# Two-layer mLSTM block on one core: the 512 tokens of x in four chunks of 128 instead of two of 256

## The chip, the core and the metric

The program runs on one core of a Trainium2 chip. Its engines, by the names of the profile, are PE (matrix multiply, with PEld for its weight loads), DVE (vector), ACT (scalar: exponentials, copies with a scale), POOL, and SP, which here only issues DMAs. The metric is the device time of one launch in microseconds; lower is better.

## The reference, cut to what matters

Two layers of a block mix 512 tokens of `x` and 256 tokens of a prefix `ctx` (width 1024). A layer projects both with `w_in`, runs an mLSTM (4 heads of width 128, forward and backward), a Fourier mixer and a convolution, joins them with `w_out`, and adds an MLP. The mLSTM is written as a scan over chunks:

```python
D = bcum[..., :, None] - bcum[..., None, :] + li[..., None, :]      # masked to s <= t
m_t = max(bcum + m, max(D))
S   = (q k^T) * exp(D - m_t)                                        # inside the chunk
num = exp(bcum + m - m_t) * (C q) + S v                             # state C, then the chunk
den = exp(bcum + m - m_t) * (n q) + sum(S)
h   = num / max(|den|, exp(-m_t))
C_new = exp(...) * C + sum_s exp(g_s - m_new) v_s k_s^T             # state for the next chunk
```

The backward direction is the same on reversed tokens. The result doesn't depend on the chunk length (but for rounding): a longer chunk has more of `S`, a shorter one more states `C`. In the last layer only x is needed after the mLSTM, and ctx only gives its state.

## The kernel before

Tokens stand as 2 blocks of 128 of ctx and 4 blocks of x. Work is recorded layer by layer. In a layer the columns of `w_in` go by chunks of 128 (`CHUNKS`): t and a for the convolution, then q, k, o for heads 0 to 3, then the Fourier columns. The products of a chunk are L464 (three matmuls for each of 8 slices of the weight and each token range, 48 in the first layer where both ranges are needed). After the chunk o of head h a generator `mlstm(h, ...)` is staged; `advance()` (called after the next chunks) runs its first part up to the first `yield` (scores, states), then its second (outputs), then its third (transposes back, L785). `background()` slips matmuls of another projection (L248, which fill one PSUM tile over 8 steps) and, by way of the priorities, the taps of the convolution (L690, on DVE) between them.

A scheduler turns the record into a fixed order for each engine. Each engine works its list strictly in that order, and an instruction at the head of the list that has to wait holds all behind it. Tiles come from pools of a fixed size; an instruction that opens a new tile waits until the readers of the tile whose room it takes are done. The pool `aux` has 4 PSUM tiles, and all of scores, transposes, states and outputs of the mLSTM take theirs there; so do the L248 sums, one tile for a long time.

For x, a head of the kernel before does this (first part of `mlstm`):

- `mb`: running maxima, broadcast to all partitions by DMA (L828).
- L835, L841: transposes of k; ACT writes them scaled, into `kw` (ctx, L838, 4 copies) and `kx` (x, L843, 4 copies).
- L848: `qs`, 4 exponentials of 256 columns, and L850 times q.
- `weighted`, once for each chunk of 256: 6 score matmuls of 256 columns (L801, operands rounded to float32r, high and low parts), then 4 exponentials (two of 256 columns, two of 128; L811), 4 masks on POOL (L779), 4 products on DVE (L814).
- L855: state at the start of x, 4 matmuls of 129 columns, copied by ACT to `cs` (L857). L862: 4 more for the second state; DVE combines both (L866).

The second part (L884) takes for each block and direction one state matmul and one or two matmuls inside the chunk, 2.5 on average, so 20 a head for x. Ctx has 6 more in the first layer. The matmuls of L855, L862 and L884 have float32 operands; the trace shows each as two records.

Ahead of that, once a layer, four small DMAs fetch the maxima at the chunk edges from DRAM (`m0`, `m1`, L652 and L653: 4 values of 4 bytes to each of 128 partitions). DVE subtracts them for `dec` (L670).

Of the kernel before, what the change touches and what calls it, by code (L numbers as in the profile page):

```python
# [10 lines left out]
F32 = mybir.dt.float32  # L11
F32R = mybir.dt.float32r
AF = mybir.ActivationFunctionType
# [5 lines left out]
CTX = 256  # L19
# [32 lines left out]
CH = 256  # L52
# [13 lines left out]
def build(tc, a):  # L66
# [408 lines left out]
    def layer(l, res, nbg, first=None):  # L475
# [168 lines left out]
        mdv = md[l][:].rearrange("(d h) t -> h d t", d=2)  # L644


        m0 = small.tile([128, 2, 4], F32, tag="m0", name=nm("m0"))
        m1 = small.tile([128, 2, 4], F32, tag="m1", name=nm("m1"))
        dec = small.tile([128, 2, 4], F32, tag="dec", name=nm("dec"))
        wx = small.tile([128, 4, 4], F32, tag="wx", name=nm("wx"))  # L650
        for d, t0, t1 in ((0, CTX - 1, CTX + CH - 1), (1, 0, CTX + CH)):
            dma(m0[:, d, :], md[l][4 * d:4 * d + 4, t0].partition_broadcast(128))  # L652
            dma(m1[:, d, :], md[l][4 * d:4 * d + 4, t1].partition_broadcast(128))  # L653

        def gate_columns():
            for q in range(2):
                ps = aux()
                for i in range(3):
                    T.transpose(ps[:, 128 * i:128 * i + 128], pm[:, 128 * (3 * q + i):128 * (3 * q + i) + 128], ident)
                v4 = ps[:, :384].rearrange("p (b g d n) -> p b g d n", b=3, g=2, d=2)  # L660
                for i in range(3):
                    V.tensor_copy(pcol[:, 3 * q + i], v4[:, i, 0, :, 0:4])
                    S.activation(em[:, 3 * q + i], v4[:, i, 1, :, 0:4], AF.Exp, scale=-1.0)
            for j in range(CB):
                V.tensor_tensor(wc[:, j], pcol[:, j], m0, ALU.subtract)
            S.activation(wc, wc, AF.Exp)
            for i in range(4):
                V.tensor_tensor(wx[:, i], pcol[:, CB + i, i // 2], m1[:, i // 2], ALU.subtract)
            S.activation(wx, wx, AF.Exp)
            V.tensor_tensor(dec, m0, m1, ALU.subtract)  # L670
            S.activation(dec, dec, AF.Exp)

        y = {}
# [117 lines left out]
        def mlstm(h, q, k, to):  # L791
            y[h] = t3()
            groups = []
            qh, ql, kh, kl = [t3(F32R) for _ in range(4)]
            i0 = XQ if last else 0
            for src, hi, lo in ((q, qh, ql), (k, kh, kl)):
                split(src[:, i0:QW], hi[:, i0:QW], lo[:, i0:QW], True)

            def scores(out, kc, q0, n):
                for i, (kp_, qp) in enumerate(((kh, qh), (kh, ql), (kl, qh))):  # L800
                    T.matmul(out, kp_[:, kc:kc + 128], qp[:, q0:q0 + n], start=i == 0, stop=i == 2)  # L801

            def weighted(mb, kc, q0, blk):

                qk = aux()
                E = t4().rearrange("p (j d t) -> p j d t", j=2, d=2)
                for j in range(2):
                    scores(qk[:, CH * j:CH * j + CH], kc + 128 * j, q0, CH)
                for j, d in ((0, 0), (0, 1), (1, 0), (1, 1)):
                    lo, hi = (128 * j, CH) if d == 0 else (0, 128 * j + 128)  # L810
                    S.activation(E[:, j, d, lo:hi], mb[:, d, lo:hi], AF.Exp, scale=-1.0,  # L811
                                 bias=pcol[:, blk + j, d, h:h + 1])
                    masked(E[:, j, d, 128 * j:128 * j + 128], d == 0)
                    V.tensor_tensor(E[:, j, d, lo:hi], E[:, j, d, lo:hi], qk[:, CH * j + lo:CH * j + hi], ALU.mult)  # L814
                return E

            def within(E, b, blk, d):
                i = b - blk
                js = range(0, i + 1) if d == 0 else range(i, 2)
                return [(E[:, j, d, 128 * i:128 * i + 128], vt[h][:, blk + j, :]) for j in js]  # L820

            if not last:
                mb = c2().rearrange("p (d t) -> p d t", d=2)
                dma(mb, mdv[h, :, 0:CTX].partition_broadcast(128))
                Ec = weighted(mb, 0, 0, 0)
                groups.append((0, range(CB), lambda b, d: within(Ec, b, 0, d)))
            mb = t4().rearrange("p (d t) -> p d t", d=2)
            dma(mb, mdv[h, :, CTX:TOK].partition_broadcast(128))  # L828

            kt = t4()  # L830
            kw = kt[:, 0:512].rearrange("p (d j n) -> p d j n", d=2, j=CB)
            kx = kt[:, 512:1024].rearrange("p (i n) -> p i n", i=4)
            kp = aux()
            for j in range(CB):
                T.transpose(kp[:, 128 * j:128 * j + 128], k[:, 128 * j:128 * j + 128], ident)  # L835
            for d in range(2):
                for j in range(CB):
                    S.activation(kw[:, d, j, :], kp[:, 128 * j:128 * j + 128], AF.Copy, scale=wc[:, j, d, h:h + 1])  # L838
            kp = aux()
            for i in range(4):  # L840
                T.transpose(kp[:, 128 * i:128 * i + 128], k[:, XQ + 128 * i:XQ + 128 * i + 128], ident)  # L841
            for i in range(4):
                S.activation(kx[:, i, :], kp[:, 128 * i:128 * i + 128], AF.Copy, scale=wx[:, i, h:h + 1])  # L843
            qs = t4().rearrange("p (d t) -> p d t", d=2)
            for d in range(2):
                for c in range(2):
                    m_ = m0 if c == d else m1
                    S.activation(qs[:, d, CH * c:CH * c + CH], mb[:, d, CH * c:CH * c + CH], AF.Exp, scale=-1.0,  # L848
                                 bias=m_[:, d, h:h + 1])
            V.tensor_tensor(qs, qs, q[:, XQ:XQ + SEQ].unsqueeze(1).to_broadcast([128, 2, SEQ]), ALU.mult)  # L850
            Ex = [weighted(mb[:, :, CH * c:CH * c + CH], XQ + CH * c, XQ + CH * c, CB + 2 * c) for c in range(2)]
            cp = aux()
            for d in range(2):
                for j in range(CB):
                    T.matmul(cp[:, 129 * d:129 * d + 129], kw[:, d, j, :], vt[h][:, j, :], start=j == 0, stop=j == CB - 1)  # L855
            cs = c2()[:, :258]
            S.activation(cs, cp[:, :258], AF.Copy)  # L857
            cp = aux()
            for d in range(2):
                for j in range(2):  # L860
                    i = 2 * d + j
                    T.matmul(cp[:, 129 * d:129 * d + 129], kx[:, i, :], vt[h][:, CB + i, :], start=j == 0, stop=j == 1)  # L862
            cs1 = c2()[:, :258]
            for d in range(2):
                dd = slice(129 * d, 129 * d + 129)
                V.scalar_tensor_tensor(cs1[:, dd], cs[:, dd], dec[:, d, h:h + 1], cp[:, dd], ALU.mult, ALU.add)  # L866

            def x_terms(b, d):
                s0 = 128 * (b - CB)
                c = (b - CB) // 2  # L870
                return [(qs[:, d, s0:s0 + 128], (cs if c == d else cs1)[:, 129 * d:129 * d + 129])] + \
                    within(Ex[c], b, CB + 2 * c, d)
            groups.append((CTX, range(CB, NB), x_terms))
            yield
            hns = []
            for t0, bs, terms in groups:
                hn = c2()
                ba = tiny.tile([128, 4, 2], F32, tag="ba", name=nm("ba"))
                for i, b in enumerate(bs):
                    ps = aux()  # L880
                    for d in range(2):
                        ts = terms(b, d)
                        for n, (st_, mv) in enumerate(ts):
                            T.matmul(ps[:, 129 * d:129 * d + 129], st_, mv, start=n == 0, stop=n == len(ts) - 1)  # L884
# [592 lines left out]
```

## Time and profile before

| | us |
|---|---|
| runs shown | 1517.34, 1513.02, 1516.81; median 1516.81 |
| profiled execution | 1513.57 |
| its span, first to last instruction | 1511.9 |
| PE busy | 1471.7 (97% of the span) |
| DVE, ACT, POOL busy | 1093.8 (72%), 757.9 (50%), 84.4 (6%) |

The mLSTM of the first layer lies between about 160 and 320 us, that of the last between about 995 and 1115 us. A row of a timeline may merge several equal instructions: "x12" is their number and the second column the time from the first start to the last end, so that the step from one to the next is that time less the length of one, over the number less one, or simply the distance to the next row over the number. The records of PE and ACT overlap: the next instruction starts before the one ahead of it has ended.

### The profile page before, as it was taken

What the parts mean: (1) busy time and instruction counts of PE and PEld (TensorE: products, weight loads), DVE (VectorE), ACT (ScalarE), POOL (GpSimd) and SP (SyncE); (2) the same over time, 40 slices, a digit from 0 to 9 for tenths busy, and PEclk for the clock granted to TensorE, in tenths of its full rate; (3) what the DMA queues carried; (4) which work ended last, traced back from release to release, by engine and by line L of the source; (5) the groups of instructions that cost most, each with busy time, mean ns of one, the idle gap of its engine ahead of it and who ended that gap; (6) DMA issues with size and microseconds to landing.
All of it is one profiled execution on the core that took longest, in us unless ns stands there. A gap on an engine that the chain in (4) does not pass through costs nothing. (4 is left out here: it accounts for less than half of the span.)

```text
span 1511.9 us, 23296 instructions
## 1 busy us (share of the span) xinstructions
PE 1471.7 (97%) x8894; PEld 1292.6 (85%) x8894; DVE 1093.8 (72%) x2155; ACT 757.9 (50%) x1523; POOL 84.4 (6%) x233
## 2 busy tenths in 40 slices
PE   7899999999999999999999999999999999999997
PEld 4878888987888898898988978888888889998887
DVE  3449987854899886766866576799666977667666
ACT  4632345535745352442524576544557555555544
POOL 0000012200000000000000010011111000000000
PEclk9999999999999999999999999999999999999999
DMA  8645436523532452432622252422225142333234
GB/s 317 156 140 206 158 122 219 207 70 123 183 126 96 144 193 72 166 136 88 195 76 92 80 183 97 133 84 76 107 84 180 43 126 98 112 112 100 83 95 143
DMA packets 68128, 197.32 MB, mean 131 GB/s; under 512 B 14064, under 2 KB 16528, under 8 KB 68016
## 3 DMA queue, kind: packets, MB, share of 16 engines
q1 hardware_dynamic: 66576, 191.11, 37.7%
q0 software_dynamic: 1440, 4.72, 1.0%
q8 instruction: 70, 1.15, 0.3%
q14 instruction: 42, 0.34, 0.1%
HBM read 183.14 MB, written 12.66 MB: 130 GB/s over the span
## 5 line engine op out<-in xcount | busy, mean ns | idle before, releaser
L220 ACT ACTIVATE hi<-raw 128x1024 fp32r<-128x1024 f32 (+1 forms) x245 | 244.0, 1000 | 375.8 <-PE mm L1074 141.6
L1074 PE MATMUL mm<-hi,t 128*128 128x512 f32 (+1 forms) x1296 | 406.4, 392 | 0.1
L221 DVE TENSOR_TENSOR lo<-raw,hi 128x1024 fp32r<-128x1024 f32 (+1 forms) x245 | 280.2, 1146 | 62.7 <-ACT hi L220 28.7
L1074 PEld LDWEIGHTS mm<-hi,t 128*128 128x128 f32 x1296 | 242.3, 188 | 54.9 <-DVE t L234 1.1
L1074 PE MATMUL mm<-lo,t 128*128 128x512 f32 (+1 forms) x648 | 253.4, 391 | 0.0
L464 PE MATMUL mm<-hhi,hi 128*128 128x256 f32 (+1 forms) x576 | 167.9, 336 | 0.0
L464 PE MATMUL mm<-hlo,hi 128*128 128x256 f32 (+1 forms) x576 | 165.8, 332 | 0.0
L464 PE MATMUL mm<-hhi,lo 128*128 128x256 f32 (+1 forms) x576 | 165.2, 331 | 0.0
L1074 PEld LDWEIGHTS mm<-lo,t 128*128 128x128 f32 x648 | 121.9, 188 | 26.3
L1143 PE MATMUL mm<-hhi,hi 128*128 128x384 f32 (+1 forms) x448 | 138.5, 309 | 1.8 <-ACT c L1169 1.7
L1143 PE MATMUL mm<-hhi,lo 128*128 128x384 f32 (+1 forms) x448 | 138.1, 308 | 1.5 <-DVE lo L221 1.5
L1242 DVE TENSOR_TENSOR t<-mm,t 128x512 f32<-128x512 f32 x120 | 81.6, 687 | 78.6 <-PE mm L1074 78.6
L1143 PE MATMUL mm<-hlo,hi 128*128 128x384 f32 (+1 forms) x448 | 138.0, 308 | 0.0
L464 PEld LDWEIGHTS mm<-hhi,hi 128*128 128x128 f32 x576 | 106.7, 188 | 14.9 <-issue 2.9
L464 PEld LDWEIGHTS mm<-hhi,lo 128*128 128x128 f32 x576 | 108.2, 188 | 10.8
L464 PEld LDWEIGHTS mm<-hlo,hi 128*128 128x128 f32 x576 | 107.8, 188 | 11.3 <-issue 0.8
L690 DVE SCALAR_TENSOR_TENSOR t<-t,half,t 128x783 f32<-128x783 f32 (+1 forms) x120 | 101.8, 886 | 0.4
L1143 PE MATMUL mm<-t,hi 128*128 128x384 f32 (+1 forms) x448 | 97.2, 308 | 0.0
L1143 PEld LDWEIGHTS mm<-hhi,hi 128*128 128x128 f32 x448 | 84.2, 188 | 3.9 <-ACT c L1169 2.2
L1143 PEld LDWEIGHTS mm<-hhi,lo 128*128 128x128 f32 x448 | 84.2, 188 | 1.9 <-DVE lo L221 1.9
L234 DVE TENSOR_TENSOR t<-c,t 128x256 fp32r<-128x256 f32 (+1 forms) x132 | 62.1, 477 | 32.5 <-ACT t L231 31.7
L1143 PEld LDWEIGHTS mm<-hlo,hi 128*128 128x128 f32 x448 | 84.2, 188 | 1.2
(254 smaller groups left out, 2706.1 us busy)
## 6 DMA issues: line engine op xcount, KB each, us to landing
raw<-w SPq DMA_DIRECT2D x128, 512.0 KB, 4.1
raw<-w_at SPq DMA_DIRECT2D x48, 512.0 KB, 3.5
raw<-w_a SPq DMA_DIRECT2D x44, 512.0 KB, 4.6
raw<-w_c SPq DMA_DIRECT2D x32, 512.0 KB, 4.2
xd<-t SPq DMA_DIRECT2D x20, 512.0 KB, 3.9
raw<-w_o SPq DMA_DIRECT2D x16, 512.0 KB, 5.3
t<-xd SPq DMA_DIRECT2D x20, 256.0 KB, 6.5
t<-x SPq DMA_DIRECT2D x8, 512.0 KB, 7.8
```

The lines of the kernel that those rows point to most:

```text
L220: S.activation(hi[:, r0:n0], raw[:, r0:n0], AF.Copy)
L221: V.tensor_tensor(lo[:, r0:n0], raw[:, r0:n0], hi[:, r0:n0].bitcast(F32), ALU.subtract)
L234: V.tensor_tensor(blk_lo, src, blk_hi.bitcast(F32), ALU.subtract)
L464: T.matmul(o[:, :n], wp[:, k, :], hp[:, k, t0:t0 + n], start=k == 0 and i == 0, stop=k == KB - 1 and i == 2)
L690: V.scalar_tensor_tensor(o, u[j][:, o0 + k:o1 + k], w, o, ALU.mult, ALU.add)
L1074: T.matmul(ps, hp[:, 128 * b:128 * b + 128], wp[:, f % 2, c0:c1], start=f == fs[0] and at[0] == 0 and n == 0, stop=f == fs[-1] and at[1] = ...
L1143: T.matmul(ps[:, :HN], wp[:, K2 * j + k, :], hp, start=first and k == 0 and i == 0, stop=k == K2 - 1 and i == 2, skip_group_check=True)
L1242: V.tensor_tensor(ac_, ps, ac_, ALU.add)
```

## The change

For x, the two chunks of 256 become four of 128, with four edges and thus a start state and three more states in each direction. The ctx part stays. What differs, a layer and head:

```diff
-        for d, t0, t1 in ((0, CTX - 1, CTX + CH - 1), (1, 0, CTX + CH)):
-            dma(m0[:, d, :], md[l][4 * d:4 * d + 4, t0].partition_broadcast(128))
-            dma(m1[:, d, :], md[l][4 * d:4 * d + 4, t1].partition_broadcast(128))
+        for n in range(4):
+            for d, t0 in ((0, CTX + 128 * n - 1), (1, TOK - 128 * n if n else 0)):
+                dma(mr[:, n, d, :], md[l][4 * d:4 * d + 4, t0].partition_broadcast(128))
...
-            V.tensor_tensor(dec, m0, m1, ALU.subtract)
+            V.tensor_tensor(dec, mr[:, 0:3], mr[:, 1:4], ALU.subtract)
...
-            for i in range(4):
-                S.activation(kx[:, i, :], kp[:, 128 * i:128 * i + 128], AF.Copy, scale=wx[:, i, h:h + 1])
+            for n in range(1, 4):
+                for d in range(2):
+                    i = after(n, d)
+                    S.activation(kx[:, n - 1, d, :], kp[:, 128 * i:128 * i + 128], AF.Copy,
+                                 scale=wx[:, n - 1, d, h:h + 1])
...
-                for c in range(2):
-                    m_ = m0 if c == d else m1
-                    S.activation(qs[:, d, CH * c:CH * c + CH], mb[:, d, CH * c:CH * c + CH], AF.Exp, scale=-1.0,
-                                 bias=m_[:, d, h:h + 1])
+                for i in range(4):
+                    S.activation(qs[:, d, 128 * i:128 * i + 128], mb[:, d, 128 * i:128 * i + 128], AF.Exp, scale=-1.0,
+                                 bias=mr[:, before(i, d), d, h:h + 1])
...
-            Ex = [weighted(mb[:, :, CH * c:CH * c + CH], XQ + CH * c, XQ + CH * c, CB + 2 * c) for c in range(2)]
+            for i in range(4):
+                scores(qk[:, 128 * i:128 * i + 128], XQ + 128 * i, XQ + 128 * i, 128)
+            for i in range(4):
+                for d in range(2):
+                    S.activation(Ex[:, i, d, :], mb[:, d, 128 * i:128 * i + 128], AF.Exp, scale=-1.0,
+                                 bias=pcol[:, CB + i, d, h:h + 1])
+                    masked(Ex[:, i, d, :], d == 0)
+            for i in range(0, 4, 2):
+                V.tensor_tensor(Ex[:, i:i + 2], Ex[:, i:i + 2], ..., ALU.mult)
...
+            S.activation(cs0, cp[:, :258], AF.Copy)
+            for n in range(1, 4):
+                cp = aux()
+                for d in range(2):
+                    T.matmul(cp[:, 129 * d:129 * d + 129], kx[:, n - 1, d, :], vt[h][:, CB + after(n, d), :],
+                             start=True, stop=True)
+                for d in range(2):
+                    V.scalar_tensor_tensor(cs[n][:, dd], cs[n - 1][:, dd], dec[:, n - 1, d, h:h + 1], cp[:, dd],
+                                           ALU.mult, ALU.add)
...
+                return [(qs[:, d, 128 * i:128 * i + 128], cs[before(i, d)][:, 129 * d:129 * d + 129]),
+                        (Ex[:, i, d, :], vt[h][:, b, :])]
```

`kw` moves to a tile of the pool `c2`, `Ex` is one tile of `t4` in place of two, and the three new states take one tile of `t3`.

The order moves with it, at three places on which the prediction rests.

PE, first layer, head 0, from the last score matmul to the last matmul of the states. `aux_1590` and `aux_1595` are the L248 sum, `mm_...` the next chunk. Before:

```order
L801 MATMUL aux_1733<-t_239_1658,t_242_1661 128x256
L855 MATMUL aux_1753<-t_57_238,t_247_1690 128x129 x4
L248 MATMUL aux_1590<-raw_1793,csil 32x256 x3
L248 MATMUL aux_1590<-raw_1799,csil 32x256 x4
L464 MATMUL mm_1811<-hhi,hi_1517 128x256
...
L862 MATMUL aux_1760<-t_57_238,t_247_1690 128x129 x4
```

With the change:

```order
L805 MATMUL aux_1725<-t_238_1663,t_241_1666 128x128
L878 MATMUL aux_1757<-t_57_238,c_246_1695 128x129 x4
L886 MATMUL aux_1765<-t_57_238,t_247_1696 128x129 x2
L248 MATMUL aux_1595<-raw_1805,csil 32x256 x3
L248 MATMUL aux_1595<-raw_1811,csil 32x256 x4
L464 MATMUL mm_1823<-hhi,hi_1522 128x256
...
L886 MATMUL aux_1770<-t_57_238,t_247_1696 128x129 x2
L464 MATMUL mm_1823<-hhi,lo_1523 128x256
L464 MATMUL mm_1824<-hhi,lo_1523 128x512
L886 MATMUL aux_1775<-t_57_238,t_247_1696 128x129 x2
```

L855 is now L878, and L862 is now L886: three pairs, each into an `aux` tile of its own. 18 matmuls of L464 stood ahead of L862; 10 stand ahead of the second pair of L886 and 2 more ahead of the third. The second pair takes the `aux` tile of L878, which ACT has to copy first.

ACT, the same head, from the copies of k to the copy of the first state. Before:

```order
L838 ACTIVATE t_247_1690<-aux_1691,wc_967 128x128 x4
L843 ACTIVATE t_247_1690<-aux_1698,wx_971 128x128 x4
L848 ACTIVATE t_250_1707<-t_246_1688,m_968 128x256
L848 ACTIVATE t_250_1707<-t_246_1688,m_969 128x256 x2
L811 ACTIVATE t_252_1714<-t_246_1688,pcol_965 128x256
L811 ACTIVATE t_252_1714<-t_246_1688,pcol_965 128x128 x2
L811 ACTIVATE t_252_1714<-t_246_1688,pcol_965 128x256
...
L857 ACTIVATE c_256_1758<-aux_1753 128x258
```

With the change:

```order
L841 ACTIVATE c_246_1695<-aux_1697,wc_967 128x128 x4
L848 ACTIVATE t_247_1696<-aux_1704,wx_970 128x128 x6
L858 ACTIVATE t_250_1715<-t_245_1693,mr_968 128x128 x8
L868 ACTIVATE t_252_1726<-t_245_1693,pcol_965 128x128 x8
L880 ACTIVATE c_254_1762<-aux_1757 128x258
```

4, 4, 4 and 8 instructions stood ahead of the copy of the state (L857); 4, 6, 8 and 8 stand ahead of it now (L880), the exponentials all of 128 columns.

SP, first layer, the DMAs around the chunk edges (`raw<-w_a` feeds L248, `raw<-w_c` a chunk). Before:

```order
L246 DMA raw_1122<-w_a 128x1024
L652 DMA m_968<-md_135 128x4x1
L653 DMA m_969<-md_135 128x4x1
...
L246 DMA raw_1128<-w_a 128x1024
L214 DMA raw_1136<-w_c 128x1024
L246 DMA raw_1193<-w_a 128x1024
```

With the change:

```order
L246 DMA raw_1125<-w_a 128x1024
L652 DMA mr_968<-md_135 128x4x1 x8
L246 DMA raw_1131<-w_a 128x1024
L214 DMA raw_1139<-w_c 128x1024
L246 DMA raw_1196<-w_a 128x1024
```

Eight edge DMAs stand in the place of four, ahead of the `raw<-w_a` of the next L248 step. On PE that step has moved too; here are the L248 steps around it, before:

```order
L248 MATMUL aux_1035<-raw_1116,csil 32x256 x4
L248 MATMUL aux_1035<-raw_1122,csil 32x256 x4
L464 MATMUL mm_1140<-hhi,hi_976 128x256
...
L248 MATMUL aux_1035<-raw_1128,csil 32x256 x4
L464 MATMUL mm_1140<-hlo,hi_976 128x256
```

and with the change:

```order
L248 MATMUL aux_1038<-raw_1119,csil 32x256 x4
L248 MATMUL aux_1038<-raw_1125,csil 32x256 x4
L464 MATMUL mm_1143<-hhi,hi_979 128x256
...
L248 MATMUL aux_1038<-raw_1131,csil 32x256 x4
L464 MATMUL mm_1143<-hlo,hi_979 128x256
```

14 matmuls of L464 stood between the second and the third step, now 26.

## Rows read from the trace of the kernel before

**Rows 1.** Section 1 of the page: busy time, share of the span, instructions.

```profile
PE 1471.7 (97%) x8894; PEld 1292.6 (85%) x8894; DVE 1093.8 (72%) x2155; ACT 757.9 (50%) x1523; POOL 84.4 (6%) x233
```

**Rows 2.** Windows view, core 0, 990 to 1030 us: busy by engine, PEclk, DMA share, GB/s.

```profile
990.00:1030.00 40.00, 37.61 (x213) 32.05 (x213) 39.09 (x86) 17.07 (x38) 6.73 (x16) 1.00 0.24 80
```

**Rows 3.** Waits of PE in the whole span: us in total, times, longest us.

```profile
PE aux L785 <- DVE c L889: 5.1, 5, 1.7
...
PE aux L801 <- DVE t L234: 0.7, 1, 0.7
```

**Rows 4.** Timeline of PE, first layer, head 0: start, us, instruction.

```profile
163.35 1.72 PE L801 MATMUL aux<-t,t 128*128 128x256 f32 x12
164.90 1.06 PE L855 MATMUL aux<-t,t 128*128 128x129 f32 x8
165.89 1.06 PE L248 MATMUL aux<-raw,csil 128*32 128x256 f32 x14
166.89 0.62 PE L464 MATMUL mm<-hhi,hi 128*128 128x256 f32 x2
...
170.12 1.05 PE L862 MATMUL aux<-t,t 128*128 128x129 f32 x8
...
176.23 1.50 PE L884 MATMUL aux<-t,t 128*128 128x129 f32 x12
177.57 0.39 PE L884 MATMUL aux<-c,t 128*128 128x129 f32 x2
```

**Rows 5.** Timeline of the weight loads ahead of 8-column matmuls.

```profile
121.88 0.52 PEld L274 LDWEIGHTS aux<-sel_sb,c 128*128 128x128 f32 x4 [0.41 <-DVE t L974]
```

**Rows 6.** Timeline of ACT, the same head.

```profile
162.56 1.16 ACT L838 ACTIVATE t<-aux,wc 128x128 f32<-128x128 f32 x4
163.55 1.20 ACT L843 ACTIVATE t<-aux,wx 128x128 f32<-128x128 f32 x4
164.55 1.78 ACT L848 ACTIVATE t<-t,m 128x256 f32<-128x256 f32 x4
166.15 2.93 ACT L811 ACTIVATE t<-t,pcol 128x256 f32<-128x256 f32 x8
168.92 0.43 ACT L857 ACTIVATE c<-aux 128x258 f32<-128x258 f32 x1
```

**Rows 7.** Timeline of ACT, last layer, head 1.

```profile
1031.63 1.13 ACT L838 ACTIVATE t<-aux,wc 128x128 f32<-128x128 f32 x4
```

**Rows 8.** Timeline of PE, last layer, head 1.

```profile
1030.75 0.60 PE L464 MATMUL mm<-hhi,hi 128*128 128x256 f32 x2
```

**Rows 9.** Timeline of DMA issues on SP, first layer.

```profile
96.64 0.42 SPq L652 DMA_DIRECT2D m<-md  x1
...
99.06 0.60 SPq L246 DMA_DIRECT2D raw<-w_a  x1
```

**Rows 10.** DMA view from 98.5 to 102.5 us: packets by size.

```profile
DMA packets 2175, 0.32 MB, mean 80 GB/s; under 512 B 2099, under 2 KB 2099, under 8 KB 2175
```

**Rows 11.** DMA view, last layer, from 971.5 to 974.6 us.

```profile
DMA packets 2216, 0.41 MB, mean 131 GB/s; under 512 B 2081, under 2 KB 2081, under 8 KB 2216
```

**Rows 12.** Timeline of PE, first layer, at the L248 step that waits.

```profile
104.47 0.64 PE L248 MATMUL aux<-raw,csil 128*32 128x256 f32 x8 [1.35 <-DMA raw<-w_a]
```

**Rows 13.** Timeline of DVE at dec, first layer.

```profile
103.08 0.17 DVE L670 TENSOR_TENSOR dec<-m,m 128x8 f32<-128x8 f32 x1 [3.70 <-DMA m<-md]
```

**Rows 14.** Timeline of DVE at dec, last layer.

```profile
975.35 0.17 DVE L670 TENSOR_TENSOR dec<-m,m 128x8 f32<-128x8 f32 x1 [1.07 <-DMA m<-md]
```

**Rows 15.** Groups of DVE by form: count, busy, mean ns, idle before.

```profile
L814 DVE TENSOR_TENSOR t<-t,aux 128x256 f32<-128x256 f32 x40 | 16.0, 416 | 3.2 <-PE aux L801 1.9 <-POOL t L779 1.3
...
L1263 DVE TENSOR_TENSOR t<-mm,t 128x512 f32<-128x512 f32 x18 | 12.1, 684 | 3.6 <-PE mm L1074 3.6
...
L814 DVE TENSOR_TENSOR t<-t,aux 128x128 f32<-128x128 f32 x40 | 9.5, 279 | 0.0
...
L866 DVE SCALAR_TENSOR_TENSOR c<-c,dec,aux 128x129 f32<-128x129 f32 x16 | 4.8, 342 | 1.4 <-PE aux L862 1.0 <-issue 0.4
```

More of the change, by code (lines that the diff above doesn't have):

```diff
@@ L644, in layer, with after @@
         mdv = md[l][:].rearrange("(d h) t -> h d t", d=2)
[L647 to L650, printed above, removed]
-        for d, t0, t1 in ((0, CTX - 1, CTX + CH - 1), (1, 0, CTX + CH)):
-            dma(m0[:, d, :], md[l][4 * d:4 * d + 4, t0].partition_broadcast(128))
-            dma(m1[:, d, :], md[l][4 * d:4 * d + 4, t1].partition_broadcast(128))
+        mr = small.tile([128, 4, 2, 4], F32, tag="mr", name=nm("mr"))
+        dec = small.tile([128, 3, 2, 4], F32, tag="dec", name=nm("dec"))
+        wx = small.tile([128, 3, 2, 4], F32, tag="wx", name=nm("wx"))
+        for n in range(4):
+            for d, t0 in ((0, CTX + 128 * n - 1), (1, TOK - 128 * n if n else 0)):
+                dma(mr[:, n, d, :], md[l][4 * d:4 * d + 4, t0].partition_broadcast(128))
+        def after(n, d):
+            return n - 1 if d == 0 else 4 - n
         def gate_columns():
@@ L664, in gate_columns @@
             for j in range(CB):
-                V.tensor_tensor(wc[:, j], pcol[:, j], m0, ALU.subtract)
+                V.tensor_tensor(wc[:, j], pcol[:, j], mr[:, 0], ALU.subtract)
             S.activation(wc, wc, AF.Exp)
-            for i in range(4):
-                V.tensor_tensor(wx[:, i], pcol[:, CB + i, i // 2], m1[:, i // 2], ALU.subtract)
+            for n in range(1, 4):
+                for d in range(2):
+                    V.tensor_tensor(wx[:, n - 1, d], pcol[:, CB + after(n, d), d], mr[:, n, d], ALU.subtract)
             S.activation(wx, wx, AF.Exp)
-            V.tensor_tensor(dec, m0, m1, ALU.subtract)
+            V.tensor_tensor(dec, mr[:, 0:3], mr[:, 1:4], ALU.subtract)
             S.activation(dec, dec, AF.Exp)
@@ L828, in mlstm @@
             dma(mb, mdv[h, :, CTX:TOK].partition_broadcast(128))
-            kt = t4()
-            kw = kt[:, 0:512].rearrange("p (d j n) -> p d j n", d=2, j=CB)
-            kx = kt[:, 512:1024].rearrange("p (i n) -> p i n", i=4)
+            kw = c2().rearrange("p (d j n) -> p d j n", d=2, j=CB)
+            kx = t4()[:, 0:768].rearrange("p (n d k) -> p n d k", n=3, d=2)
             kp = aux()
@@ L841, in mlstm, with before @@
                 T.transpose(kp[:, 128 * i:128 * i + 128], k[:, XQ + 128 * i:XQ + 128 * i + 128], ident)
-            for i in range(4):
-                S.activation(kx[:, i, :], kp[:, 128 * i:128 * i + 128], AF.Copy, scale=wx[:, i, h:h + 1])
+            for n in range(1, 4):
[3 more added lines that the diff above has]
+                                 scale=wx[:, n - 1, d, h:h + 1])
+            def before(i, d):
+                return i if d == 0 else 3 - i
             qs = t4().rearrange("p (d t) -> p d t", d=2)
             for d in range(2):
-                for c in range(2):
-                    m_ = m0 if c == d else m1
-                    S.activation(qs[:, d, CH * c:CH * c + CH], mb[:, d, CH * c:CH * c + CH], AF.Exp, scale=-1.0,
-                                 bias=m_[:, d, h:h + 1])
+                for i in range(4):
+                    S.activation(qs[:, d, 128 * i:128 * i + 128], mb[:, d, 128 * i:128 * i + 128], AF.Exp, scale=-1.0,
+                                 bias=mr[:, before(i, d), d, h:h + 1])
             V.tensor_tensor(qs, qs, q[:, XQ:XQ + SEQ].unsqueeze(1).to_broadcast([128, 2, SEQ]), ALU.mult)
-            Ex = [weighted(mb[:, :, CH * c:CH * c + CH], XQ + CH * c, XQ + CH * c, CB + 2 * c) for c in range(2)]
+            qk = aux()
+            Ex = t4().rearrange("p (j d t) -> p j d t", j=4, d=2)
+            for i in range(4):
[6 more added lines that the diff above has]
+            for i in range(0, 4, 2):
+                V.tensor_tensor(Ex[:, i:i + 2], Ex[:, i:i + 2],
+                                qk[:, 128 * i:128 * i + 256].rearrange("p (j t) -> p j t", j=2).unsqueeze(2)
+                                .to_broadcast([128, 2, 2, 128]), ALU.mult)
             cp = aux()
@@ L855, in mlstm @@
                     T.matmul(cp[:, 129 * d:129 * d + 129], kw[:, d, j, :], vt[h][:, j, :], start=j == 0, stop=j == CB - 1)
[L856 to L866, printed above, removed]
+            cs0 = c2()[:, :258]
+            S.activation(cs0, cp[:, :258], AF.Copy)
+            cx = t3()[:, :774]
+            cs = [cs0] + [cx[:, 258 * n:258 * n + 258] for n in range(3)]
+            for n in range(1, 4):
+                cp = aux()
+                for d in range(2):
+                    T.matmul(cp[:, 129 * d:129 * d + 129], kx[:, n - 1, d, :], vt[h][:, CB + after(n, d), :],
+                             start=True, stop=True)
+                for d in range(2):
+                    dd = slice(129 * d, 129 * d + 129)
+                    V.scalar_tensor_tensor(cs[n][:, dd], cs[n - 1][:, dd], dec[:, n - 1, d, h:h + 1], cp[:, dd],
+                                           ALU.mult, ALU.add)
             def x_terms(b, d):
[L869 to L872, printed above, removed]
+                i = b - CB
+                return [(qs[:, d, 128 * i:128 * i + 128], cs[before(i, d)][:, 129 * d:129 * d + 129]),
+                        (Ex[:, i, d, :], vt[h][:, b, :])]
             groups.append((CTX, range(CB, NB), x_terms))
```

## The prediction

> **What bounds the kernel now.** I read the page's first section, then the view by windows, the waits, the timelines of single heads, and at last the DMA views. PE is busy for 97% of the span [rows 1]. That is an average over all stages, so the stage of the change has to be looked at by itself: in 40 us of the last layer's mLSTM the granted clock is 1.00, and PE and DVE are both close to full [rows 2]. (PE's 37.61 there lacks some records; its timeline has no hole.) The waits of PE in the mLSTM are few: five of L785 on the copies L889, 5.1 us together, and 0.7 at L801 [rows 3]. So PE sets the end; an instruction more or less on it counts in full, work on ACT and POOL counts only where PE comes to wait for it, and DVE is near the point where it counts.
>
> All sums are made against the profiled execution, 1513.57 us. The median of the runs shown is 1516.81, 3.24 higher, and I add that at the end. Of 1516.81, 0.3% is 4.55 us; about that much can be told from no change.
>
> **float32 matmuls on PE.** Twelve records of L884 take 177.57 - 176.23 = 1.34 us [rows 4], 0.112 each, and a matmul is two records: 0.224. A head has 20 - 16 = 4 fewer of them for x in L884 and 6 - 4 = 2 more for the states: 2 fewer, 16 in the eight heads, -16 x 0.224 = **-3.6 us**. All of them stand on the bounding engine.
>
> **Score matmuls.** Twelve a head of 256 columns take 164.90 - 163.35 = 1.55, 0.129 each [rows 4]; 12 of 128 columns follow. The trace has none of that shape in float32r. Bounds: half the price, 0.056 (that of the float32 pass of 129 columns halved, or nearly half of 0.129), if columns alone count; 0.224, the price of a float32 matmul of that width, if the narrow form loses its speed. Between them lies the record of 129 columns, 0.112 [rows 4], and so do the matmuls of 8 columns, where four weight loads of 128 columns run 0.11 apart (0.52 less one load's 0.19, over three) [rows 5]: with a new weight for every matmul PE does not go below that, however few the columns. I take 0.112: 96 x (0.112 - 0.125) is **-1.2 us** (with 0.125 as the mean over several heads; 0.129 would give -1.6).
>
> The page "TensorE: Matmul & The Clock Gate" of the Trainium skill states in "LDWEIGHTS (loading the stationary operand)" a time of P/1.2 ns for P columns, which is 107 ns for 128, and the row of the loads agrees with it (0.11). In "Back-to-back issue gap" the same page has N/2.4 + 2.5 ns for a single matmul, 56 ns for 128 columns, and about 81 ns in a stream of loads and matmuls; no row here shows either. By the first the term would be -6.6 us in place of -1.2, which is rival C, by the second -4.2.
>
> **The copy of the first state, on ACT.** Here I expect the loss. In the order with the change the second pair of L886 (third pair in the other heads) opens an `aux` tile whose room is that of L878, and L878's only reader is the ACT copy L880. PE's list is strict, so all that follows, the products of the next chunk above all, waits with it. When does the copy end? ACT works its list without a hole from the first copy of k [rows 6]: copies 0.25 apart ((163.55 - 162.56)/4), exponentials of 256 columns 0.40 ((166.15 - 164.55)/4); the eight of L811 take 168.92 - 166.15 = 2.77, so the four of 128 columns take (2.77 - 1.60)/4 = 0.29. With the change 10 x 0.25 + 16 x 0.2925 + 0.43 = 7.61 us pass from the first copy of k to the end of the copy of the state, against 168.92 + 0.43 - 162.56 = 6.79. Head 0 of the first layer: 162.56 + 7.61 = 170.17. PE there: scores from 163.35, 12 x 0.112 = 1.34; L878 eight records, 0.90; first pair four records, 0.45; seven L248 in 166.89 - 165.89 = 1.00; ten L464 at (170.12 - 166.89)/18 = 0.18, 1.80; so it stands at the second pair at 168.84. Wait: 1.3 us. Before, 18 L464 stood there, and ACT was done 0.8 earlier. Head 1 of the last layer: ACT starts at 1031.63 [rows 7], the copy ends at 1039.24; PE has, from 1030.75 [rows 8], 20 L464 (3.60), the scores (1.34), L878 and two pairs (1.80): 1037.49. Wait: 1.75. In head 0 of the last layer 19 L464 of 512 columns stand ahead of the third pair, and nothing waits. In the five others it is 13 to 21 matmuls of 256 columns; I take 1.1 for each, a little less than in head 0. Sum 1.3 + 1.75 + 5.5 = **+8.5 us**. Bounds: 0, if the L464 cover it everywhere, and 8 x 1.75 = 14.
>
> This wait also makes the price of the scores nearly void: in seven heads scores that are slower than 0.112 bring PE to the same copy later, and scores that are faster bring it there sooner.
>
> What if the 128-column exponentials cost more than 0.29? They can hardly cost more than those of 256 columns, 0.40; half-way, at 0.346, the sixteen are 0.86 us longer a head, and in seven heads PE waits 6 us more: rival D.
>
> "Rules for kernel authors" of the page "ScalarE: Activation LUTs" of the Trainium skill budgets 0.3 us for an ACTIVATE and 0.83 ns for an element, 0.406 for 128 columns. By it the chain of before would have taken 8.97 us to the start of the copy, where the trace has 6.36 [rows 6], and the change would add 1.6 to it in place of 0.8. The rows don't bear it out.
>
> **The edge DMAs.** Four more a layer, each of 512 packets of 4 bytes. Before, the four are the bulk of 2099 and 2081 small packets, which take 4.0 and 3.1 us [rows 10, 11]; four issues on SP take 99.06 - 96.64 = 2.42 [rows 9]. Behind them on SP stands the `raw<-w_a` of an L248 step, and PE waited 1.35 for it at 104.47 [rows 12]. With the change it comes 3.1 to 4.0 later, and the step itself stands 12 L464 later, 12 x 0.18 = 2.15: the wait grows by 1.0 to 1.9; **+1.5 us**. Bounds 0 (the packets overlap those queued anyway) and +4 (the step's new place gains nothing).
>
> **DVE.** `dec` waits for the edges: 3.70 us idle in the first layer and 1.07 in the last [rows 13, 14], both longer by some 3 to 4 now, with 0.17 of work. In the first layer DVE has room. In the last it is 39.09 of 40 us busy [rows 2], so 1.5 us lost may come out at L801 and L785 [rows 3], which have no slack: +2. In the first layer L785 waits less, because PE comes later by the waits above: -1.5. Sum **+0.5**, bounds -1.5 and +4. The products themselves are even: before 4 x 0.416 + 4 x 0.279 + 2 x 0.342 = 3.46 us a head, after two of 512 columns, taken as the form of L1263 at 0.684, and six of 0.342: 3.42 [rows 15]. POOL's eight masks a head stay.
>
> **Sum.** -3.6 - 1.2 + 8.5 + 1.5 + 0.5 = +5.7. That is 1519.3 for the profiled execution and 1522.5 beside the median; I write 1522.
>
> **Rivals.**
> A, the forecast: PE waits for L880 in seven heads. 1522, with 1518 to 1526 as its own range. Chance 0.52; for it, the order and the unbroken ACT list.
> B, the other side: PE never waits there, because the copy is done in time. Its point: ACT has to be some 1.3 us earlier, or PE as much later, than summed. PE's stream being late (transposes, L464) while ACT starts its copies sooner would do. Then -3.6 - 1.2 + 1.5 + 0.5 = -2.8: 1514. Against it, both sides of the sum start from the same transposes. Chance 0.25.
> C, B with scores at half price: 96 x (0.056 - 0.125) = -6.6 in place of -1.2, so -2.8 - 5.4 = -8.2 and 1508.6. Against it, the loads at 0.11 [rows 5]. Chance 0.06.
> D, the longer exponentials: 1522 + 6 is 1528 to 1529. Chance 0.07.
> E, the edges reach PE in full: the L248 step late by 4 and DVE's loss in the last layer not absorbed: 1522 + 2.5 + 2 = 1527. For it, 0.24 of DMA share beside 39.09 of DVE; against it, the step's later place. Chance 0.10.
> That the change doesn't do what it says (the counts of L884 and L886 are in the order) has no chance worth a number.
>
> **Range and chances.** Faster by over 0.3% is below 1512.3: C whole and 0.08 of B, 0.14. Slower is above 1521.4: D, E and 0.33 of A, 0.50. The rest, 0.36, is within 0.3%. The range 1511.5 to 1530 leaves out C and the far ends of B and D; that of the likeliest case alone is 1518 to 1526.
>
> **What would show it.** In the profile after: a wait of PE at L886 on ACT L880 of 1 to 1.8 us in seven heads, 7 to 10 us in all, is the main step; without such a row A is wrong. The scores at L805 in steps of 0.11: at 0.056, C; at 0.22, the float32 price. ACT's rows of L858 and L868 in steps of 0.29; at 0.35 or more it is D. Some 4100 packets of under 512 bytes at 100 us, and the L248 wait there near 2.9. `dec` waiting for 5 to 7 us. DVE's groups at L785 and L805 in the waits of the last layer: over 4 us there is E. If the time is below 1512, the wait at L886 is missing or the price of a narrow matmul is not what the loads say.

## The result, and the profile after

The changed kernel took 1525.43 us (median of 4 runs, 1525.03 to 1526.86), the kernel before 1515.65 beside it: a ratio of 1.0068, 95% interval 1.005 to 1.0085, some 10 us slower. The profiled execution is the slowest of the four, 1526.86, with a span of 1525.2; that of before was among the fastest of its kernel. The two traces lie 13.3 us apart, 3.5 more than the medians, so sums made between them are a little too large.

PE is as full as before by its share:

```profile
PE 1476.1 (97%) x8862; PEld 1292.9 (85%) x8862; DVE 1097.0 (72%) x2143; ACT 765.5 (50%) x1571; POOL 90.2 (6%) x233
```

The waits of PE in the whole span, us in total, times, longest (L789 is L785 of before, L805 is L801):

```profile
PE aux L886 <- ACT c L880: 5.7, 7, 1.3
PE aux L789 <- DVE c L913: 5.2, 5, 2.6
...
PE aux L248 <- DMA raw<-w_a: 1.4, 2, 1.0
PE aux L886 <- DVE t L872: 1.4, 2, 0.7
...
PE aux L805 <- DVE t L234: 0.9, 1, 0.9
PE aux L878 <- ACT c L841: 0.9, 1, 0.9
...
PE aux L908 <- DVE t L872: 0.5, 1, 0.5
...
PE aux L726 <- DVE c L719: 0.4, 1, 0.4
...
PE aux L274 <- DVE t L872: 0.2, 1, 0.2
```

The seven stops at L886 on ACT's copy are there, one in each of seven heads, and beside them stops at L886, L878 and L908 that before didn't have. The waits of before have, besides [rows 3], the convolution's transposes L722 (L726 with the change), which lie in the same stretch:

```profile
PE aux L722 <- DVE c L715: 0.8, 1, 0.8
```

and 0.2 us more of L722 on another tile. With these all stops of PE in the stretch of the mLSTM, the L248 steps not counted, go from 6.8 to 15.2 us.

Head 0 of the first layer on PE (start, us, instruction, idle before), to be laid beside [rows 4]:

```profile
162.85 1.56 PE L805 MATMUL aux<-t,t 128*128 128x128 f32 x12
164.25 1.11 PE L878 MATMUL aux<-t,c 128*128 128x129 f32 x8
165.19 0.61 PE L886 MATMUL aux<-t,t 128*128 128x129 f32 x4
165.73 1.06 PE L248 MATMUL aux<-raw,csil 128*32 128x256 f32 x14
...
168.27 0.51 PE L464 MATMUL mm<-hlo,hi 128*128 128x256 f32 x2
169.19 0.71 PE L886 MATMUL aux<-t,t 128*128 128x129 f32 x4 [0.41 <-ACT c L880]
169.65 0.60 PE L464 MATMUL mm<-hhi,lo 128*128 128x256 f32 x2
170.97 0.71 PE L886 MATMUL aux<-t,t 128*128 128x129 f32 x4 [0.71 <-DVE t L872]
...
177.82 1.50 PE L908 MATMUL aux<-t,t 128*128 128x129 f32 x12
179.16 0.39 PE L908 MATMUL aux<-c,t 128*128 128x129 f32 x2
```

The scores take (164.25 - 162.85)/12 = 0.117 each, L908 still 1.34/12 = 0.112. The second pair of L886 stops 0.41 for the copy; the third stops 0.71 for a product of DVE. PE loses more than the idle column shows: L464 runs at 0.17 or so a step, two stand in the row at 168.27, so the next was due at about 168.62 and came at 169.19, 0.57 late where 0.41 is shown.

ACT in the same head, beside [rows 6]:

```profile
161.54 1.14 ACT L841 ACTIVATE c<-aux,wc 128x128 f32<-128x128 f32 x4 [8.42 <-PE aux L838]
162.56 1.68 ACT L848 ACTIVATE t<-aux,wx 128x128 f32<-128x128 f32 x6
164.05 2.49 ACT L858 ACTIVATE t<-t,mr 128x128 f32<-128x128 f32 x8
166.39 2.47 ACT L868 ACTIVATE t<-t,pcol 128x128 f32<-128x128 f32 x8
168.74 0.40 ACT L880 ACTIVATE c<-aux 128x258 f32<-128x258 f32 x1
```

The 128-column exponentials stand (166.39 - 164.05)/8 = 0.2925 apart, and from the first copy of k to the end of L880 it is 7.60 us.

The DVE products that free the scores' tile:

```profile
169.25 0.69 DVE L872 TENSOR_TENSOR t<-t,aux 128x512 f32<-128x512 f32 x1 [0.92 <-POOL t L783]
170.23 0.69 DVE L872 TENSOR_TENSOR t<-t,aux 128x512 f32<-128x512 f32 x1 [0.29 <-POOL t L783]
```

Each waits for the last of POOL's masks; there are two products of 512 columns, where before eight smaller ones followed their masks one by one.

Around the edges in the first layer, the issues on SP, beside [rows 9]:

```profile
96.20 4.68 SPq L652 DMA_DIRECT2D mr<-md  x8
100.98 0.45 SPq L246 DMA_DIRECT2D raw<-w_a  x1
```

the packets from 98.5 to 106.5 us, beside [rows 10]:

```profile
DMA packets 4509, 1.28 MB, mean 160 GB/s; under 512 B 4201, under 2 KB 4201, under 8 KB 4509
```

the L248 step that waits, beside [rows 12]:

```profile
105.67 0.64 PE L248 MATMUL aux<-raw,csil 128*32 128x256 f32 x8 [0.95 <-DMA raw<-w_a]
```

and `dec` on DVE, beside [rows 13, 14], in the first layer:

```profile
104.31 0.18 DVE L674 TENSOR_TENSOR dec<-mr 128x24 f32<-128x24 f32 x1 [5.21 <-DMA mr<-md]
```

and in the last:

```profile
981.68 0.18 DVE L674 TENSOR_TENSOR dec<-mr 128x24 f32<-128x24 f32 x1 [1.08 <-DMA mr<-md]
```

The time between fixed points of PE's timeline says where it went. A layer's first stretch is from its first L464 to the first matmul of its MLP output (L1074, L1098 with the change); the rest is the MLP. In us:

| kernel | first layer | MLP | last layer | MLP and end |
|---|---|---|---|---|
| before | 348.7 | 522.1 | 235.9 | 325.6 |
| with the change | 353.7 | 522.4 | 242.1 | 327.8 |

So the last layer has the largest part, +6.2, the first +5.0, and 2.2 lies in the last MLP, which the change doesn't touch. The first layer of before is short in this trace: in the four traces of edits of that kernel (below: e4, f1, f4, h3) it took 349.8 to 351.3.

### The profile page after: what moved, and what is told of

Read it like the earlier page. It is cut to its first block, busy times and chain, and to the rows that moved or that the text cites. A ratio compares the mean times of both kernels' runs of the same rounds, so it can differ in the third digit from the quotient of the medians.

```text
span 1525.2 us, 23298 instructions
## 1 busy us (share of the span) xinstructions
PE 1476.1 (97%) x8862; PEld 1292.9 (85%) x8862; DVE 1097.0 (72%) x2143; ACT 765.5 (50%) x1571; POOL 90.2 (6%) x233
## 5 line engine op out<-in xcount | busy, mean ns | idle before, releaser
L1098 PE MATMUL mm<-hi,t 128*128 128x512 f32 (+1 forms) x1296 | 405.8, 391 | 0.0
L1098 PEld LDWEIGHTS mm<-hi,t 128*128 128x128 f32 x1296 | 242.2, 188 | 53.8 <-ACT hi L220 0.3
L1098 PE MATMUL mm<-lo,t 128*128 128x512 f32 (+1 forms) x648 | 252.7, 390 | 0.0
L464 PE MATMUL mm<-hhi,hi 128*128 128x256 f32 (+1 forms) x576 | 168.9, 337 | 0.0
L464 PE MATMUL mm<-hlo,hi 128*128 128x256 f32 (+1 forms) x576 | 166.6, 334 | 0.0
L464 PE MATMUL mm<-hhi,lo 128*128 128x256 f32 (+1 forms) x576 | 165.6, 332 | 0.0
L1098 PEld LDWEIGHTS mm<-lo,t 128*128 128x128 f32 x648 | 121.8, 188 | 26.1
L464 PEld LDWEIGHTS mm<-hhi,hi 128*128 128x128 f32 x576 | 106.2, 188 | 14.8 <-issue 2.9
L464 PEld LDWEIGHTS mm<-hlo,hi 128*128 128x128 f32 x576 | 107.5, 188 | 11.7 <-issue 0.8
L464 PEld LDWEIGHTS mm<-hhi,lo 128*128 128x128 f32 x576 | 108.0, 188 | 11.1
```

Source lines behind the costliest of these rows:

```text
L464: T.matmul(o[:, :n], wp[:, k, :], hp[:, k, t0:t0 + n], start=k == 0 and i == 0, stop=k == KB - 1 and i == 2)
L1098: T.matmul(ps, hp[:, 128 * b:128 * b + 128], wp[:, f % 2, c0:c1], start=f == fs[0] and at[0] == 0 and n == 0, stop=f == fs[-1] and at[1] = ...
```

## The experiments

I began with the theory of the prediction (R: PE stops for a room in `aux` that ACT's copy frees late). Its rival W says that the loss is in the work itself.

**The first state ahead of the exponentials** (e1_state_first):

```diff
                     S.activation(kw[:, d, j, :], kp[:, 128 * j:128 * j + 128], AF.Copy, scale=wc[:, j, d, h:h + 1])
+            cp = aux()
...
+            S.activation(cs0, cp[:, :258], AF.Copy)
             kp = aux()
...
-            S.activation(cs0, cp[:, :258], AF.Copy)
```

> The changed kernel with the ctx state computed first: the four matmuls of the first state and its ACT copy stand ahead of the copies of kx and of all exponentials; same instructions, another order. Theory R (the loss is the room in aux: the pairs L886 wait for the copy of the first state behind 24 ACT instructions, 5.7 us by the waits, and each such stop costs PE some 0.17 more than the idle shown): the waits on the copy go, about 1519 to 1520; the third pair may still wait for the scores' tile, whose products follow the masks on POOL (1.4 us before this edit). Theory W (the loss is the work itself: more and smaller instructions, more changes of kind on PE): 1524 to 1526, no gain.

1526.53 us, ratio 1.0085 (1.0072 to 1.0099), where the changed kernel had 1.0068. The stops on the copy are gone, and yet nothing is won. Waits of PE in this kernel (its L878 is L872 of the changed kernel):

```profile
PE aux L789 <- DVE c L913: 8.2, 6, 3.2
...
PE mm L930 <- DVE t L234: 1.7, 1, 1.7
...
PE aux L908 <- DVE c L719: 0.9, 1, 0.9
PE aux L711 <- DVE t L878: 0.8, 1, 0.8
...
PE aux L886 <- DVE t L890: 0.3, 1, 0.3
```

L789 now has 8.2 in place of 5.2, and there are new stops: L908 and L711, and L930 in the Fourier mixer. In sum the stops in this stretch come to 15.2 us again. R's price doesn't come out.

**Two tiles for the later states** (e2_two_state_tiles):

```diff
-            for n in range(1, 4):
+            for d in range(2):
                 cp = aux()
-                for d in range(2):
-                    T.matmul(cp[:, 129 * d:129 * d + 129], kx[:, n - 1, d, :], vt[h][:, CB + after(n, d), :],
+                for n in range(1, 4):
+                    T.matmul(cp[:, 129 * n - 129:129 * n], kx[:, n - 1, d, :], vt[h][:, CB + after(n, d), :],
...
```

> The changed kernel with the three later states in two aux tiles, one for a direction with 3 x 129 columns, in place of three tiles of 2 x 129; matmuls and DVE work as they were. Theory R: one room less is needed; in the heads without an L248 sum beside them (last layer, first layer heads 2 and 3) nothing waits any more, in heads 0 and 1 of the first layer the copy of the first state is still waited for (0.4 each or more), and the waits on L872 (1.4) go: about -6, 1519 to 1520. Theory W: 1524 to 1526.

1524.89, ratio 1.0077 (1.0064 to 1.009): no gain that can be told. The stops that name the copy fall from 5.7 to 2.7 us, and L908 stops 2.3 for the sums of the states (L890), which it did not with three tiles.

**Both** (e3_first_and_two):

> Both edits of the two kernels ahead: first state first, and two state tiles. Theory R: no wait of the pairs of states is left, 8 to 11 us less than the changed kernel, 1514.5 to 1517.5. Theory W: 1524 to 1526.

1527.56, ratio 1.009 (1.0076 to 1.0104), with no stop of the pairs at all; L908 stops 2.9 for the sums of the states.

**Control: the first edit in the kernel before** (e4_before_first):

> Control: the kernel before with its first state and that copy in the place of the first edit, ahead of the copies of kx. There PE hardly waits for that copy (0.2 us once), so by theory R and by theory W alike the time is that of before, 1514 to 1518; a gain as large as in the edit of the changed kernel would say that the place of the copy helps for another reason than the wait.

1517.26, ratio 1.0028 (1.0017 to 1.004). The early copy doesn't help there either: it costs 0.2 to 0.4%, with no stop there to be won. If it costs as much in the changed kernel, it may hide some 4 us of gain in the two kernels that have it (e1, e3); the one with two tiles alone (e2) is free of this.

The traces then showed something outside the mLSTM: matmuls of the MLP, equal in both kernels, stood further apart. The larger `mr`, `dec` and `wx` push all later pools 320 bytes further in SBUF. Four kernels tested that.

**Before, 320 bytes further** (f1_before_shift320; f4_before_shift64 has 6 in place of 14, so 64 bytes):

```diff
-        wx = small.tile([128, 4, 4], F32, tag="wx", name=nm("wx"))
+        wx = small.tile([128, 14, 4], F32, tag="wx", name=nm("wx"))[:, 0:4]
```

> The kernel before with nothing changed but 160 bytes a buffer of unused room in the pool small: the order of every engine is the same, and all pools behind it (raw, whi, wlo, t4, t3, c2) lie 320 bytes further, where the change put them. Behind it is what the profile after showed outside the mLSTM: matmuls of 384 columns in the MLP, which the change doesn't touch, stand 176.8 ns apart in place of 173.4, and the second MLP is 2 us longer. Theory A (addresses): the MLP's steps go to 176 to 177 here too, and the time rises by 3 to 6 us, 1517 to 1520. Theory W (the loss is in the mLSTM's work and waits alone): 1514, and steps of 173 to 174.

> The kernel before with the pools behind small 64 bytes further, order unchanged. Theory A doesn't say which places are the good ones; a change of the MLP's steps by 1 ns or more, up or down, would show that a place matters at this distance too; steps of 173 to 174 and 1514 that 64 bytes don't. Theory W: 1514.

1517.78, ratio 1.0011 (0.9999 to 1.0023), and 1516.74, 1.0009 (0.9995 to 1.0023). The steps did move, in both: the matmuls of `hlo` by `hi` in the first MLP stand 176.7 ns apart on average, start to start, where before had 173.4. The groups of these matmuls by form (busy, and the mean length of one in ns, which grows as the steps do), before:

```profile
L1143 PE MATMUL mm<-hlo,hi 128*128 128x384 f32 x224 | 75.3, 336 | 0.0
```

and 320 bytes further:

```profile
L1143 PE MATMUL mm<-hlo,hi 128*128 128x384 f32 x224 | 75.9, 339 | 0.0
```

In the time it is 0 to 0.2%: the intervals touch 1. Nor is the first MLP itself longer: 522.1 us before, 522.7 and 522.0 in these two.

**The changed kernel with the pools in their old places** (f2_after_old_places), and the same with two state tiles (f3_two_tiles_old_places):

```diff
-    c2p = pool("c2", C2)
+    c2p = pool("c2", C2); edge = pool("edge", 2)
...
-        dec = small.tile([128, 3, 2, 4], F32, tag="dec", name=nm("dec"))
+        dec = edge.tile([128, 3, 2, 4], F32, tag="dec", name=nm("dec"))
```

> The changed kernel in its own order, with dec and wx in a pool laid out last and mr in the 160 bytes that m0, m1, dec and wx had: raw, whi, wlo, t4, t3 and c2 lie where they lay before the change. Theory A: the MLP's steps go back to 173 to 174, the time falls by 3 to 6 us, 1519.5 to 1522. Theory W: 1525.

> The changed kernel with the later states in two aux tiles, and the pools in the old places as in the kernel ahead. Theory A: 1518 to 1521.5, 3 to 6 us below the same kernel in the new places (1524.9), and a microsecond or so below the one ahead. Theory W: 1524 to 1526.

1526.29, ratio 1.0075 (1.0054 to 1.0096): the steps fell back to 174.6, the time didn't fall. With two state tiles 1523.24, 1.0049 (1.0031 to 1.0067), the best of the complete changed kernels, still slower than before. That is 0.28% below the same kernel in the new places (1.0077), a little more than the two intervals leave to noise, so a gain by the place isn't excluded there. The place is not the main cause.

Next I put theory M beside R: a stop taken away at one hand-over comes back at the next.

**The states later** (h1_states_later):

```diff
+            prio = tc.cur_priority
             for n in range(1, 4):
                 cp = aux()
+                tc.cur_priority = prio + 60
                 for d in range(2):
...
```

> The changed kernel with the three pairs of states put later in the order by their priority (24 matmuls of L464 ahead of the first pair in place of 0 in head 0, 26 in head 1, 42 and 29 in heads 0 and 1 of the last layer); nothing else changes. Theory R (PE's stop at the pairs for ACT's copy of the first state is the loss): no stop at the pairs, 6 to 8 us less than the changed kernel's 1525.4, 1517.5 to 1519.5. Theory M (each head has a chain through ACT, POOL and DVE with a fixed number of hand-overs to PE, and a stop taken away at one comes back at the next): the pairs don't wait, but the outputs L912 or the transposes L789 wait more, 1524 to 1527, as with the first state first.

1528.42, ratio 1.0079 (1.0065 to 1.0094). The pairs still stop 4.0 us in all for the copy, in place of 5.7, so the edit did only part of its work, and the outputs (L912 on the states that DVE adds up) stop 4.4.

**No copy of the first state** (h2_no_copy; the ctx state is left out of the result):

```diff
-            S.activation(cs0, cp[:, :258], AF.Copy)
+            V.memset(cs0, 0.0)
```

> The changed kernel without ACT's copy of the first state: cs0 is set to zero by DVE in its place, so the state of the ctx tokens is left out of the result; its matmuls are still done, and its room in aux has no reader. Theory R: the stops at the pairs go with the copy, 6 to 8 us less, 1517.5 to 1519.5. Theory M: other hand-overs take most of it, at most 3 us less, 1522.5 to 1525.

1526.27, ratio 1.0063 (1.0048 to 1.0077) against 1.0068 for the changed kernel. By the two intervals, the gain is at most some 4 us (an estimate from them), not the 6 to 8 of theory R. This is the plainest blow to R, though not a pure one: the edit also gives DVE a small instruction a head and lets the scheduler put PE's list in another order. Waits of PE:

```profile
PE aux L789 <- DVE c L913: 6.2, 5, 2.8
...
PE aux L908 <- DVE c L719: 1.3, 1, 1.3
...
PE mm L930 <- DVE t L234: 1.2, 1, 1.2
PE aux L878 <- ACT c L841: 1.2, 1, 1.2
...
PE aux L886 <- DVE t L872: 0.9, 1, 0.9
PE aux L886 <- DVE t L890: 0.9, 1, 0.9
```

No stop names the copy. Of those shown, all but L878 name DVE.

**Before, with eight exponentials for `qs`** (h3_before_eight_exps):

```diff
-                for c in range(2):
-                    m_ = m0 if c == d else m1
+                for i in range(4):
+                    m_ = m0 if i // 2 == d else m1
...
```

> The kernel before with one part of the change: qs in eight exponentials of 128 columns a head in place of four of 256, on ACT 0.74 us more a head, six in all. There the pair L862 has 18 matmuls and 0.8 us of slack in head 0. Theory R: the slack takes it, 1515.5 to 1517. Theory M: 0.3 to 0.5 us in most heads, 1518 to 1520.

1518.67, ratio 1.0013 (1.0005 to 1.0022). The median lies in M's range, but before took 1516.10 beside it; by the ratio it is 2 us slower, between the two theories. Its stops are those of before (L785 5.3, L801 0.5) and its layers take 349.8 and 235.8, so I see no cost on PE; the 64 bytes gave nearly as much (1.0009). Not settled.

**No copy, and half the taps of the convolution** (i1_no_copy_half_taps):

```diff
-DEFER, TAPS, LATER, AHEAD, PER = 1, 7, 300, 2, 3
+DEFER, TAPS, LATER, AHEAD, PER = 1, 4, 300, 2, 3
...
-            for k in range(31):
+            for k in range(16):
```

> The kernel without the copy of the first state (1526.3), with 16 of the 31 taps of the convolution and 4 of them after each chunk of the program in place of 7: the other 15 taps are left out of the result, some 31 us of DVE's work in the first layer (30 x 1.03) and 22 in the last. With ACT's copy gone, nearly all of PE's stops in the mLSTM name DVE. Theory D (DVE is the second bound there: its list is so full that every product and normalisation comes late, and a stop taken away at ACT returns at DVE): the stops on DVE in the mLSTM, some 13 us, fall below 5, and the time by 8 to 14, to 1512 to 1518. Theory P (the stops come from the order, which puts PE's work as early as it expects the other engines to be done, whatever they have to do): they stay above 10, 1523 to 1527.

1520.13, ratio 1.0031 (1.0021 to 1.0041), 5 us below the kernel without the copy by the ratios, less than theory D asked for. The stops on DVE in the mLSTM's stretch fell from 13.5 to 9.1 us, which is between D's 5 and P's 10. The windows show that the two layers differ. In the last layer, from 1000 to 1080 us (busy of PE, PEld, DVE, ACT, POOL), before:

```profile
1000.00:1080.00 80.00, 76.86 (x477) 67.37 (x477) 70.67 (x175) 39.84 (x98) 17.45 (x49) 1.00 0.27 91
```

with the change:

```profile
1000.00:1080.00 80.00, 74.46 (x447) 63.46 (x446) 70.72 (x163) 36.98 (x98) 14.67 (x36) 1.00 0.27 89
```

without the copy:

```profile
1000.00:1080.00 80.00, 74.12 (x435) 63.63 (x433) 72.15 (x167) 35.67 (x91) 13.61 (x36) 0.98 0.28 92
```

and with half the taps as well:

```profile
1000.00:1080.00 80.00, 78.45 (x476) 67.87 (x475) 59.73 (x149) 44.53 (x115) 14.88 (x49) 1.00 0.28 93
```

PE gets 78.45 of 80 where it had 74.12, as DVE falls from 72.15 to 59.73. The last layer takes 235.1 us against 242.6 without the copy alone: 7.5 us, more than all that the change had cost there. PE's stops between the fixed points of the last layer are 4.9 us before, 10.1 with the change, 10.6 without the copy and 4.9 again with half the taps: they are 5.2 of the 6.2 us that the change costs there, and 5.7 of the 7.5 won back. The largest are the transposes L789, without the copy:

```profile
PE aux L789 <- DVE c L913: 5.4, 3, 2.8
```

and with half the taps as well:

```profile
PE aux L789 <- DVE c L913: 2.6, 4, 1.0
```

Part of the rest of the 7.5 is TensorE's clock. Without the copy PE stood still for 2.78 us at one of these stops, and the granted clock then fell from 1.00 to 0.50, the lower of its two levels (1.2 and 2.4 GHz):

```profile
1034.92 0.39 PE L789 MATMUL aux<-ident_sb,c 128*128 128x128 f32 x1 [2.78 <-DVE c L913]
```

```profile
1036.00:1038.00 2.00, 2.00 (x7) 1.53 (x6) 1.24 (x3) 1.09 (x3) 0.00 (x0) 0.50 0.00 0
```

The 0.98 of the 80 us above is this stretch; 0.02 of 80 us is 1.6, an estimate of the most that it can cost. The traces of e1, e2, e3, f2 and h1 have one such stretch in the last layer too; those of before, of the changed kernel, of f3 and of this kernel have none there. So in each of these five, and in the kernel without the copy, up to 1.6 us of what the edit won may be hidden, which alone doesn't make up R's 6 to 8.

From 160 to 240 us in the first layer, without the copy:

```profile
160.00:240.00 80.00, 78.28 (x565) 63.97 (x564) 72.17 (x181) 33.70 (x88) 12.80 (x40) 1.00 0.39 132
```

and with half the taps:

```profile
160.00:240.00 80.00, 77.71 (x546) 63.93 (x545) 45.73 (x148) 32.34 (x84) 10.60 (x40) 1.00 0.39 132
```

DVE falls by 26 of 80 us, PE gains nothing, and the first layer takes 352.7 against 352.9. So the last layer behaves as D says and the first as P says, though DVE was as full in both (72.15 and 72.17 of 80). In the last layer theory W is out as well: PE has the 8862 records of the changed kernel, and with the same stops as before, 4.9 us, the layer takes 235.1 us where before took 235.9. The kernel before wasn't run with half the taps; part of the 7.5 us might be won there too, since it has stops on DVE in [rows 3]. That the change made DVE the limit there, and not that DVE was one already, is therefore not shown. A version faster than before was not found.

## Why the prediction was right, and where not

- **Range and side** came right: 1522 against 1525.43. The number is in part luck. Its main term, +8.5, measured 5.7 in stops, and no edit that took these stops away won time. The five terms as measured (below: -3.6, -1.2, +5.7, -0.7, +0.3) make +0.5, where the kernel lost 9.8; most of the loss is in what the sum left out.
- **float32 matmuls.** L878, L886 and L908 have 64, 96 and 304 records, 464 against 496. L908 runs in steps of 0.112 as summed; L878 (0.118) and the first pair of L886 (0.135) in head 0 run a little slower.
- **Scores.** 0.117 in head 0 where 0.112 was taken, and before 0.129 [rows 4] where 0.125 was taken: 96 x (0.117 - 0.129) is -1.2, as forecast. Rival C is out. The Trainium skill's 56 and 81 ns ("TensorE: Matmul & The Clock Gate", "Back-to-back issue gap") are not what this stream shows; the load time of the same page, 107 ns, is much nearer.
- **ACT's chain.** 7.60 us against 7.61 by the sum; rival D is out. The 0.406 us that the Trainium skill budgets for such an ACTIVATE ("ScalarE: Activation LUTs", "Rules for kernel authors") is 0.2925 here.
- **The stop at the copy.** Found in seven heads, 5.7 us for 8.5, and 0.41 to 1.25 each where 1 to 1.8 was to show it. In head 0 it was 0.41 for 1.3, for the most part because ACT began 1.31 us ahead of the scores (161.54 to 162.85) and not 0.79 as before. What failed is the step from the stop to the time: "so all that follows waits with it" was counted as a loss that would not be there without it. With the copy gone (ratio 1.0063), moved (1.0085) or given room (1.0077) no gain is seen against 1.0068. What the traces show in its place is other stops: PE comes earlier to the next hand-over and stops there. Rival B, priced at 1514 for the case without this stop, was wrong by the same step.
- **Edge DMAs.** 4201 small packets, about 4100 forecast; `dec` waits 5.21, at the low end of 5 to 7, in the first layer, but 1.08 in the last, as before. The L248 step stopped 0.95 in place of 1.35: its transfer landed 1.2 us later (104.47 to 105.67) where 3.1 to 4.0 was summed, and PE reached the step 1.6 us later (103.12 to 104.72). +1.5 was forecast; the L248 stops fell by 0.7.
- **DVE.** By the waits that it named the term came out: L785 and L801 (now L789 and L805) stop 2.6 us before and 3.9 after in the last layer, +1.3 for +2, and 3.2 and 2.2 in the first, -1.0 for -1.5. The 3.9 stays just below the 4 that would have spoken for rival E. What it had wrong is that it priced DVE apart from the copy. In the last layer the stops at L789 grew to 5.4 with the copy gone and fell to 2.6 with fewer taps. The prediction also took the 2.39 us that PE lacks in [rows 2] for missing records; they are two stops on DVE, 0.7 at L801 [rows 3] and this one:

```profile
1027.36 0.30 PE L785 MATMUL aux<-ident_sb,c 128*128 128x128 f32 x1 [1.67 <-DVE c L889]
```

  So DVE held up PE there before the change already. My reading, which no run tests by itself, is that the change gives DVE not more work but later work: fewer, larger products that wait for all masks, and a chain of three sums of states.
- **What the sum left out.** The stops that the change adds elsewhere: L886 and L908 on DVE's products (1.4 and 0.5) and L878 (0.9). A stop cost PE about 0.16 us more than its idle time where it was measured (head 0), which over eleven more stops would be 1.8. The pools' places may be 0 to 2 us. That PE's changes between the two kinds of matmul are more is not priced by any run. How the first layer's 3 to 5 us divide between these and the order stays open.

## What to carry to other kernels

Where two engines are nearly full and all work strict lists, the waits by name don't add up to a price: take one away before you believe it. Then relieve the second engine, for its busy time alone doesn't tell: DVE had 72 of 80 us in both layers, and less work for it paid where PE had 74.12 of 80, and not where PE had 78.28. And a finer grain that saves matmuls can lose more in hand-overs between engines.

## What the runs showed that was not expected

Moving pools by 64 or by 320 bytes in SBUF lengthened the steps of the matmuls of `hlo` by `hi` (384 columns, first MLP) from 173.4 to 176.7 ns, with the same order on every engine. The first MLP did not get longer by it (522.1, 522.7 and 522.0 us), and in the kernel's time it is 0 to 0.2%. The three kernels that differ in nothing else had medians of 1515.5, 1516.7 and 1517.8 us, so an effect below 0.2% of an edit that also resizes a tile can be its address.
